# Scores of 64 features: the second of two products on 128 rows instead of 64

## The chip, the core and the metric

One core of a Trainium2 chip runs the whole program. The metric is the device time of one execution in microseconds; lower is better. The core's engines are TensorE (PE for its matmuls, PEld for its weight loads), VectorE (DVE), ScalarE (ACT), GpSimd (POOL) and SyncE (SP), which issues most transfers.

## What is computed

Two layers of a block with three token mixers side by side on 256 latent and 256 context tokens of 1024 features: a gated linear attention (GLA, 4 heads), a differential attention (8 heads) and a multi-head latent attention (MLA, 8 heads). Their gated outputs are merged and projected, and a SwiGLU feed-forward follows. The second layer produces outputs for the 256 latent tokens only. The change concerns the scores of two of the mixers:

```python
def diff_core(q, k, v, lam):
    s = jnp.einsum('bhmqd,bhmkd->bhmqk', q, k)          # m = 2 maps, d = 64
    p = jax.nn.softmax(s.astype(jnp.float32), axis=-1)
    w = p[:, :, 0] - lam * p[:, :, 1]
    return jnp.einsum('bhqk,bhkd->bhqd', w.astype(v.dtype), v)

def mla_core(q_nope, q_rope, k_nope, k_rope, v):        # d = 128 and d = 64
    s = jnp.einsum('bhqd,bhkd->bhqk', q_nope, k_nope) + jnp.einsum('bhqd,bkd->bhqk', q_rope, k_rope)
    ...
```

Latent queries see 512 keys, context queries the 256 of the context.

## The kernel before

Operands of matmuls are pairs: a float32 value is split into a high half, rounded to the matmul's type float32r, and a low half, the rest. A product of two pairs takes three matmuls into one PSUM tile, high by high, high by low and low by high (`mm3`, L234 to L236). The weights stream in by 512 KB transfers (tile `raw`); ScalarE makes their high half `wh` (L212), VectorE the low half `wl` (L213), and three tiles of each are in stock.

Scores of 64 features (both maps of a differential head; the rotary part of a latent-attention head) take two matmuls instead of three. `stack_k` lays the key's high half in one group of 64 rows and its low half in the other (tiles `ks[0]`, `ks[1]`, for the map of either group). `stack_q` lays the query's high half in both groups, twice 64 rows by ScalarE (L503, L504, tiles `qs[0]`, `qs[1]`), and its low half, by VectorE (L505), in one tile `qs[2]` in the place of its own group. `stacked` then makes the score: the first matmul (L508) contracts 128 rows and gives high by high and high by low in one; the second (L509) contracts the 64 rows of one group, the query's low half by the key's high half. In the code, q of a differential head is tag `q`, the key tag `k`; in the latent attention the query's rotary part is tag `rs` and the key's tag `qr`.

`diff_proj` and `mla_proj` project a head's operands (rotation by `rope`, L483 to L486) and call `stack_q` once for the latent tokens and, in layer 0, once more for the context; in the latent attention two heads share one call. `diff_attend` and `mla_attend` take the scores for each tile of 128 queries, then the row maximum (L721), the exponential (L723), the transposes (L732, L928) and the product with the values (L785). A differential head ends with a norm by token (L790, the power on GpSimd L178, L795) and a transpose (L798). Between the heads stand parts of the branch products (`branch_part`, eviction into U, L964), gates and the projections of the next head. The order on each engine is set by a scheduler when the program is built, from dependences, buffers and its own costs; each engine then runs its list in that order, and waits where an operand isn't there.

Of the kernel before, what the change touches and what calls it, by code (L numbers as in the profile page):

```python
# [38 lines left out]
def r32(ap):  # L39
    return ap.bitcast(F32)  # L40
# [3 lines left out]
def hybrid_block_kernel(  # L44
# [18 lines left out]
    BUFS = dict(X=3, XL=3, A=3, Y=15, U=8, M=16, acc=8, a2r=2, a2=2, early=4, xt=2, raw0=11, raw1=5, u=27, wo=33, q=6, k=6, v=16, e=6, pT=11, rt=5, mr=3, mz=8, qr=2, rs=8, gt=6, o=3)  # L63
# [26 lines left out]
    def keep(shape):  # L90
        """Columns of the store for what stays for the whole program."""
        n = math.prod(shape[1:])
        o = stored[0]
        stored[0] += n
        t = store[:, o:o + n]
        if len(shape) == 3:
            t = t.rearrange("p (a b) -> p a b", b=shape[2])
        elif len(shape) == 4:
            t = t.rearrange("p (a b c) -> p a b c", b=shape[2], c=shape[3])
        return t  # L100
# [5 lines left out]
    def small(w=1):  # L106
        """w columns for values that are needed soon and briefly."""
        o = small_n[0]
        if o + w > SMALL:
            o = 0  # L110
        small_n[0] = o + w
        return ring[:, o:o + w]
# [8 lines left out]
    # the first transfers of a queue leave in the order given here  # L121
# [35 lines left out]
    # silu(c) and silu(c_ctx) as columns, the rest of the 32 columns zero  # L157
# [17 lines left out]
    def rpow(o, v, a):  # L175
        """o = (v + a) ** -0.5 on a column."""
        ts(o, v, a, None, op0=ALU.add)  # L177
        nc.gpsimd.tensor_tensor(o, o, mhalf, op=ALU.pow)  # L178

# [1 line left out]
    def load(src, kt, n, tag=None):  # L181
        """[kt * 128, n] of a weight, at most 1024 values to a partition."""
        if tag:
            return fetch(T([P, 1024], tag), src, kt, n)
        with tc.high_priority():
            return fetch(wp.tile([P, 1024], F32, tag="raw", name=nm("raw"), bufs=4), src, kt, n)
# [11 lines left out]
    def split(v, tag=None):  # L198
        """v [128, a, b] -> hi, lo as lists of a views [128, b]: products read them by k."""
        a, b = v.shape[1], v.shape[2]  # L200
        step = a if a * b <= 512 else a // 2
        hs, ls = [], []
        with tc.high_priority():
            for o in range(0, a, step):
                n = step * b
                if tag:
                    h, lo = T([P, 512], tag, F32R), T([P, 512], tag, F32R)
                else:
                    h = wp.tile([P, 512], F32R, tag="wh", name=nm("wh"), bufs=WB)
                    lo = wp.tile([P, 512], F32R, tag="wl", name=nm("wl"), bufs=WB)  # L210
                h, lo = [t[:, 0:n].rearrange("p (k c) -> p k c", c=b) for t in (h, lo)]
                nc.scalar.copy(h, v[:, o:o + step, :])  # L212
                tt(lo, v[:, o:o + step, :], r32(h), op=ALU.subtract)  # L213
                hs += [h[:, k, :] for k in range(step)]
                ls += [lo[:, k, :] for k in range(step)]
        return hs, ls
# [4 lines left out]
    def wtiles(src, kt, cols):  # L221
        """Column ranges of a [kt * 128, .] weight side by side."""
        n = sum(b - a for a, b in cols)
        with tc.high_priority():
            raw = wp.tile([P, 1024], F32, tag="raw", name=nm("raw"), bufs=4)
            v = raw[:, 0:kt * n].rearrange("p (k c) -> p k c", c=n)
            o = 0
            for a, b in cols:
                nc.sync.dma_start(v[:, :, o:o + b - a], src[:, a:b].rearrange("(k p) c -> p k c", p=P))
                o += b - a  # L230
        return split(v)
# [6 lines left out]
    def feat_block(o, w, X, n0, n1, c0=0, m=P):  # L238
        """o[m, n] = sum_k w[k, c0:c0+m]^T X[k, n0:n1]"""
        wh, wl = w  # L240
        for k in range(KD):
            mm3(o, wh[k][:, c0:c0 + m], wl[k][:, c0:c0 + m], X[k][0][:, n0:n1], X[k][1][:, n0:n1],
                k == 0, k == KD - 1)

    def wfeat(src):
        """A [1024, 128] weight."""
        tick()
        return wtile(src, KD, P)

    def wtok(src, tag=None):  # L250
        """A [1024, 256] weight as two halves of k."""
        tick()
        tick()
        return [wtile(src[512 * j:512 * j + 512, :], 4, 256, tag) for j in range(2)]

    def tok_block(o, ws, X, t0, c0, c1):
        """o[128 tokens, c1-c0] = X[:, t0:t0+128]^T w[:, c0:c1], k in order of ws"""
# [8 lines left out]
    # chunks of w_mod: 0 sh1, 1 sc1, 2 g1, 3 sh2, 4 sc2, 5 g2  # L266
# [5 lines left out]
    def mod_load(l, ch, pc, j, tag=None):  # L272
        """512 rows of 256 columns."""
# [3 lines left out]
    def mod_first(ch, pc, raws):  # L277
        """256 columns of a chunk of layer 0, both streams, by token; eight k tiles on four column groups."""
# [10 lines left out]
    def mod_step():  # L289
        """A quarter of a piece: 512 columns of a chunk, both streams, by token; each 128 have a column group."""  # L290
# [18 lines left out]
    def mod_close():  # L309
        """Columns of mcols[l, ch], bias added (+1 for scales, /2 for gates)."""  # L310
# [43 lines left out]
    def gate_rows(l, ch, s):  # L354
        """[128 tokens, 1024] of stream s's half gate, in two tiles."""
        return bcast_row(grow[l, ch][s], "v")

# [16 lines left out]
    def modulate(src, i, l, which, X):  # L374
        """src [128, 1024] tokens of tile i -> X hi/lo columns of tile i."""
# [19 lines left out]
    class Feat:  # L395
        """Feature-major hi/lo operand of 1024 features; [k] is the pair of tile k."""
# [16 lines left out]
    def first_X():  # L413
        """The first modulated operand, feature tile by feature tile as their shifts and scales come."""
# [25 lines left out]
        # the statistics of a tile run while the power of the one before is taken  # L440
# [36 lines left out]
    def rope(pl, f=1.0):  # L477
        """pl: [128, 256] PSUM of two 64-row groups -> f times the rotated."""
# [10 lines left out]
    # scores of 64 features in two products: hi twice with hi over lo, lo with hi  # L489
    ROWS = (slice(0, 64), slice(64, 128))  # L490

    def stack_k(src, ks, c):
        """ks[m]: hi of row group m in its place, lo in the other group."""
# [5 lines left out]
    def stack_q(src, qs, c, f=1.0):  # L499
        """qs[m]: hi of row group m in both groups; qs[2]: lo in place."""  # L500
        for m in range(2):
# [3 lines left out]
            stt(qs[2][r, c], src[r, :], f, r32(qs[m][r, c]), op0=ALU.mult, op1=ALU.subtract)  # L505

    def stacked(o, m, qs, q, ks, k, start, stop):
        mm(o, qs[m][:, q], ks[m][:, k], start=start, stop=False)  # L508
        mm(o, qs[2][ROWS[m], q], ks[m][ROWS[m], k], start=False, stop=stop)  # L509
# [9 lines left out]
    def gla_gates(l, X, tag, after):  # L519
        """log-decays (x 16) of all heads: {(head, dir)}: [128, 512]."""  # L520
        # one product of 96 rows: hi and lo of the weights with hi, hi with lo
# [77 lines left out]
    def gla_attend(l, h, X, TQ, la, kqv, y):  # L599
        """TQ tokens with outputs; the context's final states serve the latent part."""  # L600
        kk, qq, vv = kqv
        # running sums: bf inclusive, cb exclusive, each stream from its own start
# [8 lines left out]
        # final states of the context  # L611
# [21 lines left out]
        # queries against those states  # L633
# [9 lines left out]
        # pair weights by halving: level g pairs the halves of blocks of 2 g tokens  # L643
# [43 lines left out]
        # outputs by token, normalised  # L687
# [15 lines left out]
        for j in range(2):  # L703
            # gate
# [32 lines left out]
    def diff_proj(l, h, X, TQ, vprev):  # L737
# [8 lines left out]
        qp = [*pair("q", TQ), T([P, 512], "q", F32R)]  # L746
# [16 lines left out]
    def diff_attend(l, h, TQ, kqv, y):  # L763
        kp, qp, vv = kqv
        j = h % 2
        if True:
            ot = T([P, 512], "o")
            on = [ot[:, P * i:P * i + P] for i in range(TQ // P)]
            for i in range(TQ // P):
# [17 lines left out]
                # o / s0, then the rms norm: the scale s0 moves into its guard  # L787
# [16 lines left out]
    def mla_front(l, X, TQ):  # L804
        """normalised q and kv latents and the rotated key part, feature-major hi/lo, by token pairs."""
# [56 lines left out]
    def mla_proj(l, h, TQ, front, prev):  # L862
# [19 lines left out]
        if j == 0:  # L882
# [3 lines left out]
            qr = [*pair("rs", TQ), T([P, 512], "rs", F32R)]  # L886
# [15 lines left out]
    def mla_attend(l, h, TQ, kr, kqv, y):  # L902
# [4 lines left out]
        for i0 in range(0, TQ // P, 2):  # L907
# [14 lines left out]
            # keys by partition, both query tiles side by side  # L922
# [24 lines left out]
    def branch_part(l, br, p, y, TQ, U):  # L947
        """U (+)= rows w p .. w p + w - 1 of a branch's product, all columns; w is 512 for the short stream."""
# [17 lines left out]
    def merge(l, br, n, X, TQ, U, acc, XM, gt):  # L966
        """acc (+)= the gated branch, both twice too large"""
# [11 lines left out]
    def residual(l, i, r, G, Bt, st):  # L979
        """r <- LN(r) * G + Bt in place; st: statistics of its four column blocks."""  # L980
# [7 lines left out]
    # what runs between the heads: branch parts, gates, the latents of the MLA branch  # L988
# [92 lines left out]
    for l in range(DEPTH):  # L1081
# [68 lines left out]
        # output projection and residual  # L1150
# [16 lines left out]
        for g in groups:  # L1167
            for cb_ in range(4) if g is groups[0] else (3, 2, 1, 0):
                # the last column blocks stay for the other tokens
# [17 lines left out]
        # feed-forward  # L1187
# [13 lines left out]
        for lo_f, hi_f in (((0, RND), (RND, 22)) if TQ == 512 else ((0, 22),)):  # L1201
# [13 lines left out]
            for part in parts:  # L1215
                for cb_ in range(4) if 0 in part else (3, 2, 1, 0):
                    tags = [t for t in ("mm", "t", "s", "o") for _ in range(PB[t])][4 * (cb_ % 2):]
                    pos = {i: ps(tags[n], [P, 256]) for n, i in enumerate(part)}
                    # the last column blocks stay for the other tokens
# [13 lines left out]
                    if last and cb_ == 3:  # L1233
                        # the first tokens end early, so that only the others' norm is left at the end
# [36 lines left out]
def _constants():  # L1271
    """Arrays that the shapes alone fix: identity, rotary tables, pair masks, row selectors."""
# [41 lines left out]
```

## Time and profile before

| | |
|---|---|
| median of 3 runs | 2157.45 us (2156.32 to 2159.31) |
| span of the profiled execution | 2154.1 us |
| TensorE matmuls busy | 2099.5 us (97%) |
| VectorE busy | 1436.7 us (67%) |
| ScalarE busy | 1076.6 us (50%) |
| differential heads, layer 0 | about 314 to 618 us |
| latent-attention heads, layer 0 | about 618 to 860 us |
| differential heads, layer 1 | about 1530 to 1760 us |
| latent-attention heads, layer 1 | about 1760 to 1860 us |

The profile is of one execution. Its span runs from the first to the last instruction; the time of a run also holds what lies around the span. Matmuls overlap, each one's end being modelled, so a busy TensorE does not say how fast it advances: that is read from the starts of successive matmuls. Idle time of an engine that others don't wait for costs nothing.

### The profile page before, as it was taken

To read this page: it belongs to the slowest core of one execution; us is meant where nothing else is said; L and a number is where in the kernel's file an instruction comes from. 1 tells how busy PE (TensorE), PEld (TensorE's weight loads), DVE (VectorE), ACT (ScalarE), POOL (GpSimd) and SP (SyncE) were. 2 spreads that over 40 slices of the span, in tenths; PEclk is the share of its full clock that TensorE was granted. 3 is DMA by queue.
4 is the path that set the end of the run, shared out by engine and by line. 5 is a ranking of instruction groups with operands and counts; after the bars stand their busy time and mean duration, and the time that the engine had idled before them with its cause. 6 is when DMAs were issued, how large, how long until landed. Compare 5 with 4: busy or idle time off the path is not lost.

```text
span 2154.1 us, 36382 instructions
## 1 busy us (share of the span) xinstructions
PE 2099.5 (97%) x14103; PEld 1812.2 (84%) x14103; DVE 1436.7 (67%) x3168; ACT 1076.6 (50%) x2495; POOL 96.0 (4%) x187
## 2 busy tenths in 40 slices
PE   7999999999999999999999999999999999998998
PEld 4888887777777778799899889988978888998998
DVE  5699657767467666685334448598566888785656
ACT  3756345666454553434231334765465676644452
POOL 0001001111000000010000000000000000000000
PEclk9999999999999999999999999999999999998999
DMA  9322343332322234627324446533434333568653
GB/s 294 102 87 69 118 99 93 86 106 60 91 81 66 78 127 137 176 84 214 104 89 127 118 127 182 159 91 118 136 88 128 106 113 85 172 191 213 172 178 116
DMA packets 349270, 268.29 MB, mean 125 GB/s; under 512 B 19932, under 2 KB 316520, under 8 KB 349096
## 3 DMA queue, kind: packets, MB, share of 16 engines
q1 hardware_dynamic: 335632, 252.22, 40.1%
q10 hardware_dynamic: 13464, 13.74, 2.1%
q8 instruction: 111, 1.82, 0.3%
q14 instruction: 63, 0.52, 0.1%
HBM read 263.79 MB, written 2.12 MB: 123 GB/s over the span
## 4 chain that ended last, share of the span: by engine, by line
PE 79%; DVE 11%; ACT 4%; issue 2%; POOL 2%; DMA 1%; ACTq 0%; DVEq 0%; POOLq 0%
PE ps_mm L234 18%; PE ps_mm L235 18%; PE ps_mm L236 18%; PE ps_s L234 3%; PE ps_s L236 3%; PE ps_s L235 3%; PE ps_s L509 3%; POOL store L178 2%; PE ps_s L508 2%; DVE wl L213 2%; PE ps_md L299 1%; PE ps_s L681 1%; DMA grow<-store 1%; ACT rt L483 1%; PE ps_t L928 1%
## 5 line engine op out<-in xcount | busy, mean ns | idle before, releaser
L213 DVE TENSOR_TENSOR wl<-raw,wh 128x512 fp32r<-128x512 f32 (+2 forms) x719 | 468.8, 674 | 139.7 <-ACT wh L212 82.4
L212 ACT CAST wh<-raw 128x512 fp32r<-128x512 f32 (+2 forms) x719 | 416.2, 611 | 254.1 <-PE ps_mm L235 135.0
L234 PE MATMUL ps_mm<-X,wh 128*128 128x512 f32 (+1 forms) x1264 | 440.8, 349 | 0.0
L235 PE MATMUL ps_mm<-XL,wh 128*128 128x512 f32 (+1 forms) x1264 | 437.4, 346 | 0.0
L236 PE MATMUL ps_mm<-X,wl 128*128 128x512 f32 (+1 forms) x1264 | 435.7, 345 | 0.0
L234 PEld LDWEIGHTS ps_mm<-X,wh 128*128 128x128 f32 x1264 | 241.2, 191 | 33.3 <-issue 7.3
L235 PEld LDWEIGHTS ps_mm<-XL,wh 128*128 128x128 f32 x1264 | 241.3, 191 | 27.3 <-issue 2.7
L236 PEld LDWEIGHTS ps_mm<-X,wl 128*128 128x128 f32 x1264 | 241.0, 191 | 26.2 <-issue 0.7
L236 PE MATMUL ps_mm<-wh,XL 128*128 128x256 f32 (+1 forms) x544 | 156.8, 292 | 0.0
L235 PE MATMUL ps_mm<-wl,X 128*128 128x256 f32 (+1 forms) x544 | 156.5, 292 | 0.1
L234 PE MATMUL ps_mm<-wh,X 128*128 128x256 f32 (+1 forms) x544 | 152.8, 294 | 0.0
L178 POOL TENSOR_TENSOR store<-store 128x1 f32<-128x1 f32 x112 | 75.6, 676 | 1657.4 <-DVE store L177 1633.9
L234 PE MATMUL ps_s<-X,wh 128*128 128x256 f32 (+1 forms) x384 | 126.2, 329 | 4.9 <-ACT wh L212 4.9
L236 PE MATMUL ps_mm<-wh,u 128*128 128x256 f32 x444 | 125.8, 283 | 0.0
L235 PE MATMUL ps_mm<-wl,u 128*128 128x256 f32 x444 | 125.6, 283 | 0.0
L234 PE MATMUL ps_mm<-wh,u 128*128 128x256 f32 x444 | 125.6, 283 | 0.0
L236 PE MATMUL ps_s<-X,wl 128*128 128x256 f32 (+1 forms) x384 | 125.1, 326 | 0.0
L235 PE MATMUL ps_s<-XL,wh 128*128 128x256 f32 (+1 forms) x384 | 125.0, 326 | 0.0
L234 PE MATMUL ps_mm<-Y,wh 128*128 128x512 f32 (+1 forms) x352 | 119.9, 341 | 0.1
L235 PE MATMUL ps_mm<-Y,wh 128*128 128x512 f32 (+1 forms) x352 | 118.6, 337 | 0.0
L236 PE MATMUL ps_mm<-Y,wl 128*128 128x512 f32 (+1 forms) x352 | 118.4, 336 | 0.0
L723 ACT ACTIVATE e<-ps_s,store 128x512 f32<-128x512 f32 (+1 forms) x144 | 88.5, 617 | 47.1 <-DVE store L721 45.4
(306 smaller groups left out, 4481.7 us busy)
## 6 DMA issues: line engine op xcount, KB each, us to landing
raw<-in_w_in_dram SPq DMA_DIRECT2D x144, 512.0 KB, 4.6
raw<-in_w_mod_dram SPq DMA_DIRECT2D x96, 512.0 KB, 3.7
raw<-in_ffn_w_in_dram SPq DMA_DIRECT2D x96, 512.0 KB, 7.1
raw<-in_w_branch_dram SPq DMA_DIRECT2D x48, 512.0 KB, 3.5
raw<-in_ffn_w_out_dram SPq DMA_DIRECT2D x46, 512.0 KB, 3.4
raw<-in_w_out_dram SPq DMA_DIRECT2D x16, 512.0 KB, 4.2
raw<-in_w_in_dram SPq DMA_DIRECT2D x16, 448.0 KB, 3.4
v<-grow ACTq DMA_DIRECT2D x12, 256.0 KB, 4.1
```

The source lines that it names most:

```text
L178: nc.gpsimd.tensor_tensor(o, o, mhalf, op=ALU.pow)
L212: nc.scalar.copy(h, v[:, o:o + step, :])
L213: tt(lo, v[:, o:o + step, :], r32(h), op=ALU.subtract)
L234: mm(o, lh, rh, start=start, stop=False)
L235: mm(o, lh, rl, start=False, stop=False)
L236: mm(o, ll, rh, start=False, stop=stop)
L299: mm(pm[32 * g:32 * g + 32, :], cst[:, 2 * j + k, :], v[:, k, P * g:P * g + P], start=(j == 0 and k == 0), stop=(j == 3 and k == 1))
L483: act(qw[a:a + 32, :], pl[b:b + 32, :], AF.Copy, scale=f)
L508: mm(o, qs[m][:, q], ks[m][:, k], start=start, stop=False)
L509: mm(o, qs[2][ROWS[m], q], ks[m][ROWS[m], k], start=False, stop=stop)
L681: mm(pa[:, i, :], kx[:, P * i:P * i + P], qx[:, P * j:P * j + P], start=True, stop=True)
L723: act(e, pscore, AF.Exp, bias=mx, accum_out=s)
```

## The change

The query's low half gets a tile for each map, `qs[2]` and `qs[3]`, and stands there in both groups of rows. The second matmul contracts all 128 rows: the query's low half by the key's high half and, new, by its low half. The tags `q` and `rs` get two buffers more each. The first matmul, the key's side and the transfers stay.

```diff
-    BUFS = dict(... q=6, ... rs=8, ...)
+    BUFS = dict(... q=8, ... rs=10, ...)
...
     def stack_q(src, qs, c, f=1.0):
         for m in range(2):
             r, o = ROWS[m], ROWS[1 - m]
             act(qs[m][r, c], src[r, :], AF.Copy, scale=f)
             act(qs[m][o, c], src[r, :], AF.Copy, scale=f)
-            stt(qs[2][r, c], src[r, :], f, r32(qs[m][r, c]), op0=ALU.mult, op1=ALU.subtract)
+            for g in (r, o):
+                stt(qs[2 + m][g, c], src[r, :], f, r32(qs[m][r, c]), op0=ALU.mult, op1=ALU.subtract)

     def stacked(o, m, qs, q, ks, k, start, stop):
         mm(o, qs[m][:, q], ks[m][:, k], start=start, stop=False)
-        mm(o, qs[2][ROWS[m], q], ks[m][ROWS[m], k], start=False, stop=stop)
+        mm(o, qs[2 + m][:, q], ks[m][:, k], start=False, stop=stop)
...
-        qp = [*pair("q", TQ), T([P, 512], "q", F32R)]
+        qp = [*pair("q", TQ), *pair("q", TQ)]
...
-            qr = [*pair("rs", TQ), T([P, 512], "rs", F32R)]
+            qr = [*pair("rs", TQ), *pair("rs", TQ)]
```

The rest of the diff takes comments out. From L506 of the changed kernel on, lines have numbers that are one higher: the subtraction is L506, the two matmuls L509 and L510.

The scheduler answers the added subtractions with another order in places. On VectorE, at the operands of the second differential head of layer 0 (`q` tiles are the query's halves, `rt` the rotated query, `ps_mm` the projection in PSUM, U the branch product, `wl` the low half of weights), before:

```order
L505 SCALAR_TENSOR_TENSOR q_3362<-ps_mm_3325,q_3360 64x256
L964 TENSOR_TENSOR U_746<-U_746,ps_mm_3411 128x512
L505 SCALAR_TENSOR_TENSOR q_3362<-rt_3363,q_3360 64x256
L964 TENSOR_TENSOR U_747<-U_747,ps_mm_3419 128x512
L505 SCALAR_TENSOR_TENSOR q_3362<-rt_3363,q_3361 64x256
L213 TENSOR_TENSOR wl_3442<-raw_3435,wh_3441 128x512
L213 TENSOR_TENSOR wl_3611<-raw_3608,wh_3610 128x512
L505 SCALAR_TENSOR_TENSOR q_3362<-ps_mm_3325,q_3361 64x256
```

and after:

```order
L506 SCALAR_TENSOR_TENSOR q_3367<-ps_mm_3330,q_3365 64x256 x2
L506 SCALAR_TENSOR_TENSOR q_3367<-rt_3369,q_3365 64x256 x2
L506 SCALAR_TENSOR_TENSOR q_3368<-rt_3369,q_3366 64x256 x2
L213 TENSOR_TENSOR wl_3452<-raw_3445,wh_3451 128x512
L506 SCALAR_TENSOR_TENSOR q_3368<-ps_mm_3330,q_3366 64x256
L213 TENSOR_TENSOR wl_3621<-raw_3618,wh_3620 128x512
L506 SCALAR_TENSOR_TENSOR q_3368<-ps_mm_3330,q_3366 64x256
L965 TENSOR_TENSOR U_746<-U_746,ps_mm_3421 128x512
L965 TENSOR_TENSOR U_747<-U_747,ps_mm_3429 128x512
```

Eight subtractions stand where four stood, and the evictions into U that stood between them now come behind.

On TensorE, at the scores of the first latent-attention head of layer 0 (three score tiles `ps_s`, the key `qr`, the query's high and low half `rs`), before:

```order
L508 MATMUL ps_s_6240<-qr_3862,rs_6187 128x512
L509 MATMUL ps_s_6240<-qr_3862,rs_6189 128x512
L508 MATMUL ps_s_6251<-qr_3862,rs_6187 128x512
L509 MATMUL ps_s_6251<-qr_3862,rs_6189 128x512
L508 MATMUL ps_s_6295<-qr_3862,rs_6187 128x256
L509 MATMUL ps_s_6295<-qr_3862,rs_6189 128x256
L234 MATMUL ps_mm_6347<-mz_3860,wh_6343 128x512
```

and after:

```order
L509 MATMUL ps_s_6285<-qr_3877,rs_6227 128x512
L509 MATMUL ps_s_6296<-qr_3877,rs_6227 128x512
L509 MATMUL ps_s_6340<-qr_3877,rs_6227 128x256
L510 MATMUL ps_s_6285<-qr_3877,rs_6229 128x512
L510 MATMUL ps_s_6296<-qr_3877,rs_6229 128x512
L510 MATMUL ps_s_6340<-qr_3877,rs_6229 128x256
L234 MATMUL ps_mm_6392<-mz_3875,wh_6388 128x512
```

The three low products, which stood each behind its high product, now stand together behind the third high product.

## Rows read from the trace of the kernel before

**Rows 1.** The page: busy time by engine, and the chain of waits by engine.

```profile
PE 2099.5 (97%) x14103; PEld 1812.2 (84%) x14103; DVE 1436.7 (67%) x3168; ACT 1076.6 (50%) x2495; POOL 96.0 (4%) x187
...
PE 79%; DVE 11%; ACT 4%; issue 2%; POOL 2%; DMA 1%; ACTq 0%; DVEq 0%; POOLq 0%
```

**Rows 2.** Busy time by stretch: window, its length, busy us (count) per engine, clock, DMA.

```profile
314.00:618.00 304.00, 298.23 (x1694) 228.16 (x1693) 208.72 (x510) 175.10 (x481) 35.75 (x72) 1.00 0.30 89
618.00:860.00 242.00, 241.49 (x1252) 190.15 (x1252) 161.69 (x326) 117.98 (x265) 0.00 (x0) 1.00 0.33 97
1530.00:1760.00 230.00, 225.84 (x1565) 192.81 (x1565) 164.31 (x378) 143.00 (x372) 18.64 (x37) 1.00 0.38 114
1760.00:1860.00 100.00, 98.60 (x663) 84.54 (x662) 83.64 (x194) 69.41 (x172) 1.47 (x3) 1.00 0.31 87
```

**Rows 3.** The chain of waits by line, in those four stretches, in their order.

```profile
by line: PE ps_mm L235 18.6%; PE ps_mm L234 18.1%; PE ps_mm L236 17.5%; PE ps_s L509 7.5%; POOL store L178 5.1%; PE ps_s L508 4.7%; PE ps_o L785 3.1%; DVE o L795 3.0%; ACT rt L483 2.2%; PE ps_md L299 1.8%; DVE pT L734 1.8%; DVE k L497 1.8%;
...
by line: PE ps_mm L234 23.5%; PE ps_mm L236 22.6%; PE ps_mm L235 22.5%; PE ps_s L509 4.9%; PE ps_t L928 4.3%; PE ps_s L234 3.2%; PE ps_s L508 2.9%; PE ps_o L234 2.8%; PE ps_o L235 2.6%; PE ps_o L236 2.3%; PE ps_s L236 2.1%; PE ps_s L235 2.0
...
by line: PE ps_mm L234 18.0%; PE ps_mm L235 17.2%; PE ps_mm L236 17.1%; PE ps_s L509 5.7%; PE ps_s L508 4.6%; ACT rt L483 3.8%; PE ps_o L785 3.2%; issue 2.2%; DVE pT L734 2.1%; DVE wl L213 2.1%; POOL store L178 2.0%; DVE k L497 1.7%; PE ps_
...
by line: PE ps_mm L234 16.3%; PE ps_mm L235 15.3%; PE ps_mm L236 15.3%; PE ps_t L928 7.0%; PE ps_s L509 6.9%; PE ps_s L508 4.9%; PE ps_o L234 4.5%; PE ps_s L236 3.9%; PE ps_o L235 3.9%; PE ps_s L235 3.6%; PE ps_s L234 3.5%; PE ps_o L236 3.3
```

**Rows 4.** Line L509, the low product: count, min/median/max ns, first and last start, forms.

```profile
L509 PE MATMUL ps_s<-k,q x96: 378/492/503, 315.3 to 1760.4; 64*128 64x512 f32 x64, 64*128 64x256 f32 x32
...
L509 PE MATMUL ps_s<-qr,rs x48: 379/492/503, 618.6 to 1852.6; 64*128 64x512 f32 x32, 64*128 64x256 f32 x16
```

**Rows 5.** Matmuls in time, 512 columns: start us, us, engine, line, tiles, rows*columns.

```profile
313.63 0.39 PE L234 MATMUL ps_mm<-Y,wh 128*128 128x512 f32 x1
...
314.99 0.39 PE L508 MATMUL ps_s<-k,q 128*128 128x512 f32 x1
315.31 0.50 PE L509 MATMUL ps_s<-k,q 64*128 64x512 f32 x1
315.74 0.49 PE L508 MATMUL ps_s<-k,q 128*128 128x512 f32 x1
...
317.45 0.50 PE L234 MATMUL ps_mm<-X,wh 128*128 128x512 f32 x1
317.79 0.40 PE L235 MATMUL ps_mm<-XL,wh 128*128 128x512 f32 x1
```

**Rows 6.** The same view, where score pairs have 256 columns.

```profile
320.25 0.28 PE L508 MATMUL ps_s<-k,q 128*128 128x256 f32 x1
...
320.77 0.50 PE L236 MATMUL ps_mm<-X,wl 128*128 128x512 f32 x1
321.10 0.39 PE L234 MATMUL ps_mm<-X,wh 128*128 128x512 f32 x1
```

**Rows 7.** All engines in time, before the first latent-attention scores.

```profile
617.64 0.40 DVE L505 SCALAR_TENSOR_TENSOR rs<-ps_mm,rs 64x256 fp32r<-64x256 f32 x1
...
618.07 0.28 PE L235 MATMUL ps_s<-k,q 128*128 128x256 f32 x1
...
618.18 0.28 PE L236 MATMUL ps_s<-k,q 128*128 128x256 f32 x1
...
618.30 0.40 PE L508 MATMUL ps_s<-qr,rs 128*128 128x512 f32 x1
```

**Rows 8.** Line L553, a product of 96 rows and 512 columns.

```profile
L553 PE MATMUL ps_s<-e,a x16: 392/395/446, 66.9 to 1384.5; 96*128 96x512 f32 x16
```

**Rows 9.** Matmuls in time, two low products side by side.

```profile
427.25 0.50 PE L509 MATMUL ps_s<-k,q 64*128 64x512 f32 x2
```

**Rows 10.** VectorE by line and form: busy us, mean ns, idle before.

```profile
L497 DVE TENSOR_TENSOR k<-rt,k 64x256 fp32r<-64x256 f32 x32 | 13.4, 419 | 0.8
L505 DVE SCALAR_TENSOR_TENSOR q<-rt,q 64x256 fp32r<-64x256 f32 x32 | 13.3, 417 | 6.2 <-ACT q L503 5.9
```

**Rows 11.** Who TensorE waited for, 314 to 618 us: total us, times, longest.

```profile
PE ps_t L798 <- DVE o L795: 3.3, 11, 0.7
```

More of the change, by code (lines that the diff above doesn't have):

```diff
@@ L61, in nm @@
         return f"{s}_{uid[0]}"
-    BUFS = dict(X=3, XL=3, A=3, Y=15, U=8, M=16, acc=8, a2r=2, a2=2, early=4, xt=2, raw0=11, raw1=5, u=27, wo=33, q=6, k=6, v=16, e=6, pT=11, rt=5, mr=3, mz=8, qr=2, rs=8, gt=6, o=3)
+    BUFS = dict(X=3, XL=3, A=3, Y=15, U=8, M=16, acc=8, a2r=2, a2=2, early=4, xt=2, raw0=11, raw1=5, u=27, wo=33, q=8, k=6, v=16, e=6, pT=11, rt=5, mr=3, mz=8, qr=2, rs=10, gt=6, o=3)
     def T(shape, tag, dtype=F32):
```

## The prediction, on record before the changed kernel ran

> **What bounds the kernel now.** I read the busy table first, then the stretches in which the changed products run, then the chain of waits, and last the matmuls one by one. TensorE is busy for 97% of the span, VectorE for 67% [rows 1]. The changed products lie in four stretches: the differential heads of layer 0 (314 to 618 us), its latent-attention heads (618 to 860), and the same two of layer 1 (1530 to 1760, 1760 to 1860). In each, TensorE is idle for 5.8, 0.5, 4.2 and 1.4 us, some 12 us in all, and VectorE is busy for 208.7 of 304, 161.7 of 242, 164.3 of 230 and 83.6 of 100 us [rows 2]. So TensorE sets the pace there, and the only stretch in which VectorE comes near it is the last (84%). The chain of waits agrees: the low product of the scores (L509) alone holds 7.5%, 4.9%, 5.7% and 6.9% of these stretches [rows 3], that is 22.8 + 11.9 + 13.1 + 6.9 = 54.7 us.
>
> **What the low product costs now.** There are 96 + 48 = 144 of them, all of 64 rows; 96 have 512 columns, 48 have 256 [rows 4]. A busy TensorE hides their price, since matmuls overlap; it is seen from start to start. Six 128-row products of 512 columns in a row start 1.36 us apart in all, 0.227 each (313.63 to 314.99). Then three score pairs (high product L508, low product L509) follow: 314.99, 315.31, 315.74, and so on to 317.45, and the matmul behind them starts its successor at 317.79 [rows 5]. These seven intervals take 2.80 us where seven at 0.227 would take 1.59. So 1.21 us are lost over three pairs, 0.40 a pair. With 256 columns: the intervals from 320.25 to 321.10 take 0.85 us [rows 6]; two products of 256 columns start 0.23 us apart in all (618.07 to 618.30, [rows 7]), so these two and one of 512 would take 0.46, and 0.39 us is lost. The loss lies on both sides of the 64-row product: it starts 0.1 us late, the product behind it 0.2 us late, the next 0.1.
>
> Is it the short contraction? A product of 96 rows and 512 columns lasts 395 ns [rows 8], like the 128-row ones in [rows 5], while a 64-row one lasts 492 [rows 4]. So it isn't; what costs is going from products on the whole array to one on a half and back. The new low product has 128 rows, reads the same key tile as the high product before it and writes the same bank; I take 0.227 and 0.115 us for it, as for every 128-row product.
>
> **The sum on TensorE.** In layer 0 each differential head scores two latent query tiles against 512 keys and two context tiles against 256, twice (64 products, half and half); the latent-attention heads do it once (32, half and half); layer 1 has 32 + 16, all against 512. So 96 x 0.403 + 48 x 0.39 = 57.4 us. By stretch that is 25.4, 12.7, 12.9 and 6.4 us. At three places two low products stand next to each other and share the way there and back; one is shown in [rows 9]. They lose some 1.2 us less, so 56 us.
>
> One more row bears on this. At 427.25 us two low products, of the two row groups, take 0.50 us together [rows 9]. The Trainium skill, TensorEngine Tiling (Array Packing), Key Properties, says that tiles of the array work independently and that different tiles can run matmuls in parallel; by it the way to use 64-row products is to set two of different groups side by side, and the change, against that rule, gives it up. The trace agrees at that place, but two 128-row products take 2 x 0.227 = 0.45 us, which is no more; and the order of the kernel before sets them so at one place of 144, so the sum stays at 56 us.
>
> **What it adds on VectorE.** The query's low half is written to both row groups: four subtractions (L505, now L506) instead of two for each call of stack_q. There are 72 now, of 0.417 us [rows 10], and 72 more come, 30.2 us; the order of the changed kernel shows the doubled rows. The new ones read one row group and write the other. The row nearest to that is L497 of the key, which does just this in 0.419 us [rows 10], so they are no dearer. By stretch: 32 x 0.42 = 13.4, 6.7, 6.7 and 3.4 us. With TensorE's saving taken off the stretch, VectorE would be busy for 222 of 279 us (80%), 168 of 229 (73%), 171 of 217 (79%) and 87 of 93.5 us (93%). So the added work lies beside TensorE's, except where VectorE is itself on the chain: it holds 11% of the whole chain [rows 1], so 30.2 x 0.11 = 3 us, with 0 and 30 us as the ends. What is queued behind the new rows is the splitting of the next weights (L213) and the evictions into U, as the order shows in the second head; TensorE waits for those when VectorE falls behind by more than the three split tiles that are in stock. ScalarE gets no work, and no transfer moves; the added buffers (two of tag q, two of tag rs) cost no time.
>
> At the first latent-attention head all four of the first subtractions come before the low products. In the trace the first of them starts at 617.64; two more behind it end by 617.64 + 3 x 0.42 = 618.9, and the three high products from 618.30 on end their starts at 618.30 + 0.57 = 618.87 [rows 7]. So hardly a wait there.
>
> **What is late next.** With the scores done earlier, TensorE comes to the steps that hang on the softmax sooner. The longest of its waits now is for the normalised outputs of the differential heads (L798 for L795): 3.3 us over 11 in the first stretch [rows 11]. All its waits in the four stretches come to 12 us. Lower end: none grow, since VectorE and ScalarE start the softmax sooner too. Upper end: in the differential heads half the saving is waited away, (25.4 + 12.9) / 2 = 19 us. I take 8 us, nearer to the waits that are there than to the upper end, because both sides of that chain move forward.
>
> **The forecast.** -56 + 3 + 8 = -45 us. The profiled execution has a span of 2154.1 us; the median of the runs is 2157.45, so 3.4 us lie outside the span, and they stay. 2154.1 - 45 + 3.4 = **2112.5 us**, 2.1% faster.
>
> **Rivals.**
> (a) The softmax chain takes over in the differential heads: 19 us of waits instead of 8, and 10 us of VectorE's rows on the chain. -56 + 19 + 10 = -27, **2130 us**. For it: in these heads the chain also runs through L795, L734 and the one-column powers of GpSimd (POOL store L178, 5.1%, [rows 3]). Against it: TensorE waits only 5.8 of 304 us there [rows 2].
> (b) VectorE becomes the bound: all 30.2 us exposed, -56 + 30 = -26, **2131 us**. For it: 93% in the last stretch. Against it: that stretch holds only 3.4 us of the added work; elsewhere a fifth of VectorE's time is left.
> (c) The new order also removes some of the 12 us of waits: all 57 us and a few more, **2095 us**.
> (d) Slower: the price isn't the half array but the second product itself, that is reading the same keys again into the same bank. Then the second product still costs 0.40 us with 128 rows, TensorE saves nothing, and VectorE adds its 30.2 us, a third of which would be exposed next to a TensorE that is as slow as now: **2167 us**. It decides if the matmul behind the new low product still starts 0.43 us after it. Against it: the three products of mm3 also fill one bank, the third (L236 at 618.18) reads the key tile of the first again, and they keep 0.115 us [rows 7].
> (e) Next to no change: a small saving and small waits cancel, **2157 us**; nothing in the profile calls for it.
>
> **Chances.** The forecast, from 36 to 57 us saved: 0.68. (a) 0.13, (b) 0.07, (c) 0.05, (d) 0.04, (e) 0.03. A measurement of this kernel tells changes of about 0.2% (4 us) from none. Faster by more: 0.68 + 0.13 + 0.07 + 0.05 = 0.93; within: 0.03; slower: 0.04. The range takes in the full saving with nothing lost and a little luck (2157.45 - 59 = 2098) and (a) and (b) at its upper end, 2131.
>
> **What would show it.** Right: the low product on 128 rows, starting 0.227 us after the high one, and the matmul behind it 0.227 later; the four stretches shorter by about 23, 12, 10 and 5 us, nothing changed elsewhere; 144 subtractions of 0.42 us; VectorE near 80% in the differential heads, near 93% in the last stretch; TensorE's waits in the four stretches at about 20 us instead of 12. Wrong: starts still 0.3 to 0.43 us apart around the low product (d); waits of 30 us or more at L798, L785 and L732, now one line further down (a); waits of TensorE for the splits of L213 (b).

## The result, and the profile after

| | before | after |
|---|---|---|
| median | 2157.07 us | 2119.92 us (4 runs, 2118.81 to 2120.92) |
| span of the profiled execution | 2154.1 us | 2117.7 us |
| ratio of the times | | 0.9828 (95% interval 0.9817 to 0.984) |

The kernel became 1.7% faster: 37 us were gained, 45 had been forecast. The time is inside the range and 7.4 us above the forecast.

The first view is the page: busy time by engine, and the chain of waits by engine.

```profile
PE 2052.3 (97%) x14103; PEld 1808.8 (85%) x14103; DVE 1461.3 (69%) x3240; ACT 1073.1 (51%) x2495; POOL 98.2 (5%) x187
...
PE 77%; DVE 12%; ACT 5%; issue 2%; POOL 2%; DMA 1%; ACTq 0%; DVEq 0%; POOLq 0%; SPq 0%
```

Against [rows 1] TensorE's matmuls lost 47 us of busy time, VectorE gained 25 us and 72 instructions, and VectorE's share of the chain of waits rose by a point. The next view is the matmuls in time (start us, us, engine, line, tiles, rows*columns), at the scores that [rows 5] and [rows 6] show of before; L509 is now the high product, L510 the low one.

```profile
315.92 0.39 PE L509 MATMUL ps_s<-k,q 128*128 128x512 f32 x1
316.14 0.39 PE L510 MATMUL ps_s<-k,q 128*128 128x512 f32 x1
316.37 0.39 PE L509 MATMUL ps_s<-k,q 128*128 128x512 f32 x1
316.60 0.39 PE L510 MATMUL ps_s<-k,q 128*128 128x512 f32 x1
...
317.27 0.39 PE L234 MATMUL ps_mm<-X,wh 128*128 128x512 f32 x1
...
319.54 0.28 PE L509 MATMUL ps_s<-k,q 128*128 128x256 f32 x1
319.65 0.28 PE L510 MATMUL ps_s<-k,q 128*128 128x256 f32 x1
319.77 0.40 PE L236 MATMUL ps_mm<-X,wl 128*128 128x512 f32 x1
```

High and low products start 0.227 us apart, and the matmul behind a pair 0.227 us after it. With 256 columns it is 0.11 to 0.12 us. At these places no trace is left of the 0.40 us that a pair lost.

The rows of the weight loads (PEld) show what the loss went with. In the kernel before, at the first pair of [rows 5]:

```profile
314.77 0.19 PEld L508 LDWEIGHTS ps_s<-k,q 128*128 128x128 f32 x1
315.31 0.18 PEld L509 LDWEIGHTS ps_s<-k,q 64*128 64x128 f32 x1 [0.35 <-issue]
315.74 0.19 PEld L508 LDWEIGHTS ps_s<-k,q 128*128 128x128 f32 x1 [0.25 <-issue]
```

The load for the 128-row product at 314.99 starts 0.22 us ahead of it; the load for the 64-row product at 315.31 starts with it, and so does the next one, for the 128-row product at 315.74. Over all 144 low products the median lead of the load is 0.002 us before the change and 0.223 us after it.

In the chain of waits of the first stretch the change reads so (line by line, shares of the stretch):

```profile
by line: PE ps_mm L234 17.8%; PE ps_mm L235 17.6%; PE ps_mm L236 17.3%; POOL store L178 5.3%; PE ps_o L786 4.3%; PE ps_s L509 3.6%; PE ps_s L510 3.5%; DVE o L796 3.0%; ACT rt L483 2.8%; issue 2.4%; PE ps_md L299 2.4%; DVE k L497 2.1%; ACT e
```

L509 and L510 now hold about the same there, where the low product held 7.5% against 4.7% of the high one [rows 3].

For a comparison by stage I cut each trace at the same matmuls: the first score product of the differential heads of a layer, the first of its latent-attention heads, and the first eviction of the output projection behind these (L1158 of before), so that the latent-attention stages also hold what stands between the heads and that projection. Busy time in these four stages, in the columns of [rows 2] (length, then busy us of PE, PEld, DVE, ACT, POOL), before:

```profile
314.99:618.30 303.31, 297.54 (x1691) 227.66 (x1690) 208.03 (x509) 174.67 (x481) 35.75 (x72) 1.00 0.31 89
618.30:908.29 289.99, 284.22 (x1487) 225.27 (x1486) 190.09 (x371) 138.74 (x302) 0.00 (x0) 0.99 0.37 108
1565.91:1770.49 204.58, 199.38 (x1349) 167.24 (x1348) 152.47 (x353) 131.53 (x345) 18.04 (x37) 1.00 0.34 103
1770.49:1918.56 148.07, 147.94 (x1087) 135.45 (x1088) 118.41 (x259) 95.95 (x224) 0.55 (x1) 1.00 0.52 154
```

and after:

```profile
315.92:600.53 284.61, 276.13 (x1691) 226.17 (x1690) 217.22 (x537) 173.73 (x481) 36.09 (x72) 1.00 0.34 96
600.53:882.51 281.98, 272.93 (x1485) 223.03 (x1484) 195.00 (x388) 137.50 (x302) 0.00 (x0) 0.99 0.38 111
1541.08:1735.50 194.42, 187.66 (x1349) 167.75 (x1347) 156.96 (x367) 131.16 (x345) 19.84 (x37) 1.00 0.37 110
1735.50:1882.85 147.35, 144.84 (x1087) 135.53 (x1088) 122.06 (x267) 95.16 (x224) 0.55 (x1) 1.00 0.54 156
```

The stages became 18.7, 8.0, 10.2 and 0.7 us shorter, 37.6 us in all; the rest of the program is 1.3 us longer. TensorE's idle time in them (length less PE busy) rose from 5.8 + 5.8 + 5.2 + 0.1 = 16.9 us to 8.5 + 9.0 + 6.8 + 2.5 = 26.8. So the score products became as cheap as forecast, and part of the gain came back as waiting.

### The profile page after: what moved, and what is told of

Same layout as the page of the kernel before. It is cut to its first block, busy times and chain, and to the rows that moved or that the text cites. A ratio compares the mean times of both kernels' runs of the same rounds, so it can differ in the third digit from the quotient of the medians.

```text
span 2117.7 us, 36478 instructions
## 1 busy us (share of the span) xinstructions
PE 2052.3 (97%) x14103; PEld 1808.8 (85%) x14103; DVE 1461.3 (69%) x3240; ACT 1073.1 (51%) x2495; POOL 98.2 (5%) x187
## 4 chain that ended last, share of the span: by engine, by line
PE 77%; DVE 12%; ACT 5%; issue 2%; POOL 2%; DMA 1%; ACTq 0%; DVEq 0%; POOLq 0%; SPq 0%
PE ps_mm L234 18%; PE ps_mm L235 18%; PE ps_mm L236 18%; PE ps_s L234 3%; PE ps_s L236 3%; PE ps_s L235 3%; POOL store L178 2%; DVE wl L213 2%; PE ps_md L299 2%; PE ps_s L682 1%; ACT rt L483 1%; PE ps_s L509 1%; PE ps_s L510 1%; PE ps_o L786 1%; ACT wh L212 1%
## 5 line engine op out<-in xcount | busy, mean ns | idle before, releaser
L213 DVE TENSOR_TENSOR wl<-raw,wh 128x512 fp32r<-128x512 f32 (+2 forms) x719 | 468.4, 674 | 143.1 <-ACT wh L212 70.7
```

## Experiments

**Theories.** T1, that of the forecast: the gain is the end of the 64-row products (56 us), the waits take back some 8 us, and the added work of VectorE is nearly free (3 us). T2: the added subtractions cost far more than 3 us, because TensorE waits for VectorE. T3, the rival (d): it isn't the rows of the second product that cost. Eight kernels tell them apart. Some compute what the kernel before computes, some also low by low, like the changed one. The kernel before ran beside them, with 2156.84 us (e1, e2, e3, e6) and 2156.01 us (e5, e7, e8, e9).

The scheduler orders each kernel anew, so a run differs from its neighbour in the order of some instructions too; no run holds the order fixed. All results in one table: the change of each stage against before, in us, read from the same landmarks in each trace. Differential heads are D0 and D1, latent-attention heads M0 and M1, for the two layers.

| kernel | median us | ratio (95%) | D0 | M0 | D1 | M1 | elsewhere |
|---|---|---|---|---|---|---|---|
| after | 2119.92 | 0.9828 (0.9817 to 0.984) | -18.7 | -8.0 | -10.2 | -0.7 | +1.3 |
| e1_zero | 2111.12 | 0.9792 (0.9777 to 0.9806) | -20.4 | -11.0 | -11.2 | -2.7 | +0.4 |
| e2_dve_only | 2167.39 | 1.0051 (1.0034 to 1.0068) | +2.2 | +3.6 | +1.1 | +2.4 | +1.6 |
| e3_side_by_side | 2138.23 | 0.9918 (0.9903 to 0.9932) | -14.8 | +2.6 | -7.6 | +1.0 | +1.6 |
| e5_pool_copy | 2111.60 | 0.9793 (0.9778 to 0.9807) | -20.5 | -10.6 | -10.7 | -2.9 | -0.2 |
| e6_ring1 | 2131.41 | 0.9891 (0.9876 to 0.9905) | -17.4 | -7.2 | -11.4 | -2.8 | +14.0 |
| e7_diff_only | 2129.03 | 0.9876 (0.986 to 0.9893) | -18.9 | +0.4 | -10.2 | 0.0 | +0.7 |
| e8_mla_zero | 2114.39 | 0.9807 (0.9792 to 0.9821) | -18.8 | -12.1 | -10.2 | -2.6 | +0.8 |
| e9_zero_early | 2114.25 | 0.9804 (0.9789 to 0.9818) | -20.1 | -10.8 | -10.8 | -2.4 | 0.0 |

**e2: the subtractions alone.** The added subtractions of VectorE stay, the 64-row product comes back.

```diff
-        mm(o, qs[2 + m][:, q], ks[m][:, k], start=False, stop=stop)
+        mm(o, qs[2 + m][ROWS[m], q], ks[m][ROWS[m], k], start=False, stop=stop)
```

> VectorE's part of the change alone: the low half is written to both row groups, but the second product reads the 64 rows of one group as before. Theory A: TensorE is slower here than in the changed kernel and hides more of the added 30 us, so 2158 to 2165 us. Theory B: 2156 to 2159 us, as before. If the second product, and not its 64 rows, were what costs, the changed kernel's gain would have another cause and show here: 2120 us.

It took 10.5 us more than the kernel before, more than any of the expectations allowed; 9.3 of them lie in the four stages, 6.0 in the two of the latent attention, which hold 24 of the 72 added instructions. So VectorE's work costs 10 us, not 3, on a TensorE that is as slow as before. The forecast had this price, a third of the added work, in its rival (d), and this run came at that rival's time. And what the changed kernel gains over this one, 47.5 us, is the 128-row product alone: T3 falls, since by it the two would be equal.

**e1: zeros instead.** The low half stands only in its own group, the other group is set to zero by GpSimd, and the product still runs over 128 rows. VectorE has the work of before.

```diff
-            for g in (r, o):
-                stt(qs[2 + m][g, c], src[r, :], f, r32(qs[m][r, c]), op0=ALU.mult, op1=ALU.subtract)
+            nc.gpsimd.memset(r32(qs[2 + m][o, c]), 0.0)
+            stt(qs[2 + m][r, c], src[r, :], f, r32(qs[m][r, c]), op0=ALU.mult, op1=ALU.subtract)
```

> The changed kernel with the low half subtracted into its own row group only, as before the change, and zeros set by GpSimd in the other group; the second product keeps 128 rows. It computes what the kernel before computes. VectorE's 72 added subtractions are gone, TensorE's side of the change stays. Theory A (TensorE gains about 48 us from the 128 rows, and some 10 us of that are lost to VectorE's added work): faster than the changed kernel, 2107 to 2113 us. Theory B (the lost part is the wait on the softmax chain alone, VectorE's added work costs nothing): as the changed kernel, 2118 to 2122 us.

This kernel is 8.8 us faster than the changed one, and 45.7 us faster than the kernel before. It is, with e5, the fastest of the study and computes what the kernel before computes. The work that VectorE gave up stands on GpSimd, as the groups of its page show (engine, operation, tile, shape, count, then busy us and mean ns of one; what comes behind is idle time before them):

```profile
L505 POOL MEMSET q<- 64x256 f32 x48 | 13.8, 305 | 1.7
L505 POOL MEMSET rs<- 64x256 f32 x24 | 7.1, 312 | 179.4 <-PE ps_o L236 94.6 <-DVE k L515 42.2 <-PE ps_mm L235 40.7
```

These are 20.9 us on an engine that is busy for 5% of the span. Its four stages, in the columns of before:

```profile
314.83:597.73 282.90, 275.62 (x1691) 226.15 (x1690) 206.20 (x509) 173.97 (x481) 44.62 (x104) 1.00 0.35 97
597.73:876.73 279.00, 272.47 (x1483) 223.45 (x1482) 188.48 (x372) 137.50 (x302) 3.77 (x14) 0.99 0.40 113
1536.03:1729.37 193.34, 187.62 (x1349) 167.80 (x1347) 151.12 (x353) 130.58 (x345) 22.20 (x53) 1.00 0.37 109
1729.37:1874.75 145.38, 144.28 (x1087) 136.05 (x1088) 118.13 (x259) 95.49 (x224) 2.38 (x7) 1.00 0.54 158
```

In them e1 against after gives the price of VectorE's work once more: 1.7, 3.0, 1.1 and 2.0 us, 7.7 in all (by the unrounded lengths), and again most of it, 4.9, in the latent attention.

**e5: a copy by GpSimd.** Does it matter that the second place is filled later, or that VectorE fills it? Here it is filled with the low half, as in the changed kernel, but by a copy of GpSimd behind VectorE's subtraction.

```diff
-            for g in (r, o):
-                stt(qs[2 + m][g, c], src[r, :], f, r32(qs[m][r, c]), op0=ALU.mult, op1=ALU.subtract)
+            stt(qs[2 + m][r, c], src[r, :], f, r32(qs[m][r, c]), op0=ALU.mult, op1=ALU.subtract)
+            nc.gpsimd.tensor_copy(qs[2 + m][o, c], r32(qs[2 + m][r, c]))
```

> The changed kernel, with the second place of the low half copied by GpSimd from the first instead of subtracted again by VectorE; it computes what the changed kernel computes. If it is VectorE's time that the added subtractions cost: as the run with zeros, 2109 to 2114 us. If it is their lateness, that is the longer way from the projection to the second product, the copy lengthens that way further: 2118 to 2124 us.

```profile
L506 POOL CAST q<-q 64x256 fp32r<-64x256 f32 x48 | 25.9, 545 | 120.6 <-DVE q L505 106.3 <-issue 13.1 <-POOL store L178 0.8
...
L506 POOL CAST rs<-rs 64x256 fp32r<-64x256 f32 x24 | 9.9, 415 | 202.6 <-DVE rs L505 189.2 <-PE ps_t L929 12.5 <-PE ps_t L799 0.9
```

Its copies start behind the subtractions and take 0.42 to 0.55 us, and the kernel is as fast as with zeros (2111.60 and 2111.12). The expectation took the second place to be later than in the changed kernel. It isn't: it is ready 0.64 us behind the first subtraction on average, against 0.74 there, since there the second subtraction often waits for its turn on VectorE (for the context's queries of the latent attention the medians are 0.50 and 1.14). What the run shows is that a second place that comes 0.64 us behind the first costs no more than zeros, which don't wait for the subtraction. So most of the 8 to 9 us goes with the work on VectorE; that none of it is lateness isn't shown for the latent attention's context.

**e7 and e8: where VectorE's time counts.** e7 changes the differential heads only; the latent attention keeps three tiles and its 64-row product.

```diff
...
-            qr = [*pair("rs", TQ), *pair("rs", TQ)]
+            qr = [*pair("rs", TQ), T([P, 512], "rs", F32R)]
```

`stack_q` and `stacked` do as before where they are given three tiles.

> The change in the differential heads alone; the latent-attention heads keep their 64-row product and one low half. From the stretches of the changed kernel (differential heads 18.7 and 10.2 us shorter, latent-attention heads 8.0 and 0.8): 2126 to 2131 us. If the latent-attention heads' share were not worth its subtractions at all: 2118 to 2121 us.

Its differential heads are those of the changed kernel (-18.9 and -10.2), its latent attention that of before (+0.4 and 0.0). So the stages don't act upon each other here, and the latent attention's part of the change is worth 9.1 us against 18.7 (12.6 + 6.1) that its low products cost. e8 puts zeros there alone, and leaves the doubled subtraction to the differential heads.

```diff
...
-            stack_q(rope(pq[:, 0:256]), qr, slice(0, 256))
+            stack_q(rope(pq[:, 0:256]), qr, slice(0, 256), zeros=True)
...
-                stack_q(pq[:, 256:512], qr, slice(256, 512))
+                stack_q(pq[:, 256:512], qr, slice(256, 512), zeros=True)
```

> The changed kernel with zeros by GpSimd instead of the second subtraction in the latent-attention heads alone (24 of the 72 added subtractions gone; there it computes what the kernel before computes). If the added work costs most where VectorE is on the path to a short projection, as the stretches of the runs with and without it say (3.0 + 1.9 us of 7.7 there): 2114 to 2116 us. If each subtraction costs the same: 24 of 72 of 9 us, 2117 us.

It gains 5.5 us on the changed kernel with a third of the subtractions taken away (four runs, 2112.84 to 2116.17, all below the 2117 of an equal price for each). A wait that the forecast missed can be read in the trace. In the latent attention the context's half of the query is subtracted straight from the projection in PSUM (`rs<-ps_mm`). All engines in time after the first latent-attention scores of layer 0, in the changed kernel (in brackets the idle time before an instruction, and what ended it):

```profile
603.09 0.43 DVE L506 SCALAR_TENSOR_TENSOR rs<-ps_mm,rs 64x256 fp32r<-64x256 f32 x1
...
603.54 0.69 DVE L213 TENSOR_TENSOR wl<-raw,wh 128x512 fp32r<-128x512 f32 x1
...
604.27 0.43 DVE L506 SCALAR_TENSOR_TENSOR rs<-ps_mm,rs 64x256 fp32r<-64x256 f32 x1
...
604.73 0.42 DVE L515 TENSOR_TENSOR v<-ps_mm,v 128x256 fp32r<-128x256 f32 x1
...
604.75 0.50 PE L234 MATMUL ps_mm<-mz,wh 128*128 128x512 f32 x1 [1.57 <-DVE rs L506]
```

The second subtraction that reads the projection's tile stands behind the splitting of a weight (L213, 0.69 us), and the tile comes free at 604.70. TensorE, which needs it for the next projection, had been idle for 1.57 us. Among TensorE's waits of this stage (us in total, times, longest) it is the largest new one:

```profile
PE ps_mm L234 <- ACT M L514: 5.3, 2, 2.8
PE ps_mm L234 <- DVE rs L506: 1.6, 1, 1.6
PE ps_s L510 <- DVE rs L506: 0.8, 1, 0.8
PE ps_mm L234 <- DVE v L515: 0.4, 1, 0.4
```

With the wait at the scores (0.8) and the one for the values (0.4) that makes 2.8 us, about the 3.0 us by which e1 is shorter there; e1 has none of the three, and the kernel before, like all of them, has the wait for M. In e2, with the slower TensorE, the first and the third are there too:

```profile
PE ps_mm L234 <- DVE rs L506: 1.2, 1, 1.2
PE ps_mm L234 <- DVE v L515: 1.1, 2, 0.8
```

**e9: zeros once a tile.** One memset where the tile is made (64 x 512 in layer 0), instead of two of 64 x 256 in `stack_q`: are the zeros on a path?

```diff
...
-        qp = [*pair("q", TQ), *pair("q", TQ)]
+        qp = cleared([*pair("q", TQ), *pair("q", TQ)])
...
```

> As the run with zeros, but one GpSimd instruction a tile, written ahead of the subtractions and of the projection's rotation, so that the zeros wait for nothing but the tile: half as many GpSimd instructions in layer 0. If the zeros were late anywhere there: 2105 to 2109 us; if they were hidden: as that run, 2109 to 2113 us.

2114.25 us; no faster than e1, and above both ranges. Each of its four stages is within 0.5 us of e1's, so the zeros of e1 cost nothing that this could take away; the 3 us between the medians are not explained.

**e6: zeros once for all.** Two fixed tiles hold the low halves of all heads, and their zeros are set once at the start. The tags `q` and `rs` have six and eight buffers again.

```diff
...
-        qp = [*pair("q", TQ), *pair("q", TQ)]
+        qp = [*pair("q", TQ), *lows(TQ)]
...
```

> As the run with zeros, but the low halves live in two fixed tiles whose zeros are set once at the start, so neither VectorE nor GpSimd gets work for them; the price is that a head's low halves can't be written before the last head's products have read them. Theory A: 2105 to 2113 us if that wait is hidden, up to 2125 if it isn't. Theory B: 2118 to 2125 us.

It took 2131.41 us, above every range that was expected. It was meant to show what it costs when a head must wait for the tile of the last one. It doesn't: 13 us are lost before the first differential head, where none of these tiles is in use. TensorE's longest wait there, up to 330 us, is:

```profile
PE ps_s L690 <- DVE gt L718: 8.5, 1, 8.5
```

No row of the kernel before has this wait. Behind it TensorE's granted clock is 0.56 from 115.3 to 125.0 us, so for most of that stretch it is at the lower of its two levels, 1.2 GHz; the kernel before has 1.00 from 100 to 150 us. By an estimate from these numbers, 9.7 us at 0.56 lose 4.3 us, which with the wait comes to 12.8 of the 13. The fixed tiles changed the order of TensorE's products in the GLA stage, where e1 has that of the kernel before. In the four stages e6 is 6.5 us behind e1, and how much of that is the fixed tiles' wait is left open by this run.

**e3: 64 rows, side by side.** The kernel before, with one thing changed: in the differential heads both maps' high products come first, then both low products, of the two row groups, next to each other.

```diff
...
-                for m in range(2):
-                    sc = ps("s", [P, 512])[:, 0:n]
-                    stacked(sc, m, qp, slice(P * i, P * i + P), kp, slice(P * a, P * b), True, True)
-                    es.append(softmax_e(sc, n))
+                qc, kc = slice(P * i, P * i + P), slice(P * a, P * b)
+                if True:
+                    scs = [ps("s", [P, 512])[:, 0:n] for m in range(2)]
+                    tail.pop("s", None)
+                    for m in range(2):
+                        chain("s", mm(scs[m], qp[m][:, qc], kp[m][:, kc], start=True, stop=False))
+                    for m in range(2):
+                        chain("s", mm(scs[m], qp[2][ROWS[m], qc], kp[m][ROWS[m], kc], start=False, stop=True))
+                    for m in range(2):
+                        es.append(softmax_e(scs[m], n))
...
```

> The kernel before with another order only: in the differential heads the two maps' high products stand first, then their two 64-row low products next to each other (in all 48 cases), which use different row groups. If the price is the way to the half array and back, and two row groups run at the same time, a pair of pairs loses 0.40 us instead of 0.80 and gives back 0.23 (0.12 with 256 columns) by the overlap: 32 x 0.63 + 16 x 0.50 = 28 us on TensorE, of which some is lost since the second score tile must be free earlier: 2130 to 2145 us. If the 64 rows cost by themselves: 2155 to 2160 us.

```profile
316.89 0.61 PE L778 MATMUL ps_s<-k,q 128*128 128x512 f32 x2
317.44 0.50 PE L780 MATMUL ps_s<-k,q 64*128 64x512 f32 x2
317.87 0.50 PE L778 MATMUL ps_s<-k,q 128*128 128x512 f32 x1
318.20 0.39 PE L234 MATMUL ps_mm<-X,wh 128*128 128x512 f32 x1
```

Two low products take 0.50 us together (317.44), and the next matmul starts 0.43 us after the first of them. The way to the half array and back is paid once for two products and not for each. That gives 18.6 us without any work on VectorE, half of what the change gains, in 96 of the 144 products. The Trainium skill, TensorEngine Tiling (Array Packing), Key Properties, says that different tiles can run matmuls in parallel; the trace agrees, in all 48 pairs the two start within 0.01 us. But each pair still pays the way there and back, and two 128-row products, 2 x 0.227 us, are no longer than two 64-row ones side by side; with 256 columns they are shorter (0.23 us against 0.31 to 0.34). By stage the differential heads gain 22.4 us here; the rest of the program, which wasn't changed, gets 5.2 us longer, and this run doesn't show why.

## Why the prediction was right, and where its size was off

**The loss at the low product: right.** The price of 56 us was read at two places and multiplied. Summed over all 144 low products of the trace of before (from the matmul ahead of each to the second one behind it, from start to start, less 0.227 us for 512 columns, 0.120 for 256 and 0.111 for 128) it is 25.1, 12.6, 13.1 and 6.1 us in the four stages, 56.9 us. Reckoned in the same way, the changed kernel has 6.8 us at its low products, 2.3 of them waits for other engines, so some 50 us of the loss are gone; e2 against after confirms that it is the rows.

**Given back behind the saving: 8 forecast as waits, 11.6 measured.** e1 has the whole saving and no work added to VectorE. Its stages are 45.3 us shorter, so 56.9 - 45.3 = 11.6 us were given back. It isn't the differential heads' chain alone, as the forecast had it: by stage it is 4.7, 1.6, 1.9 and 3.4 us. The wait that it named did grow, but little, from 3.3 us [rows 11] to 4.0 (L799 for L796):

```profile
PE ps_t L799 <- DVE o L796: 4.0, 13, 0.8
PE ps_o L786 <- DVE pT L735: 2.4, 4, 0.9
```

Of the 11.6 us, 3.8 are idle time of TensorE in the stages of e1 (7.3 + 6.5 + 5.7 + 1.1 = 20.6 us against 16.9). The rest lies in intervals in which the modelled end of one matmul covers the start of the next, 4.0 us of it at e1's low products; which engine held them the views don't say, and that stays open. So as idle time the term was 3.8 us, below the 8 of the forecast, and what lifts it to 11.6 isn't shown to be waiting. The forecast's sign of it, about 20 us of idle time in its four stretches instead of 12, came true in the changed kernel (21.2 from 316 to 842 and 1541 to 1825), but in part by luck: 6.2 of the 9.9 us of new idle time go with VectorE's added work (26.8 us against 20.6 in e1).

**VectorE's added work: 3 forecast, 8 to 10.** This is the step that failed most. The price of one was right, with 0.42 us:

```profile
L506 DVE SCALAR_TENSOR_TENSOR q<-rt,q x64: 406/420/425, 295.6 to 1718.5; 64x256 fp32r<-64x256 f32 x64
L506 DVE SCALAR_TENSOR_TENSOR q<-ps_mm,q x32: 409/423/428, 295.1 to 544.7; 64x256 fp32r<-64x256 f32 x32
L506 DVE SCALAR_TENSOR_TENSOR rs<-rt,rs x32: 406/420/425, 600.2 to 1808.7; 64x256 fp32r<-64x256 f32 x32
L506 DVE SCALAR_TENSOR_TENSOR rs<-ps_mm,rs x16: 406/422/428, 599.9 to 744.3; 64x256 fp32r<-64x256 f32 x16
```

What was wrong is the 11%, VectorE's share of the whole chain, taken for every place. e1 against after gives 8.8 us, e2 against before 10.5. In the differential heads the 48 added instructions, 20.1 us of work, cost 2.8 to 3.3 us by stage, 14 to 16%: there the share was nearly right. In the latent attention 24 of them, 10.1 us of work, cost 4.9 to 6.0 us, half or more. The forecast looked for the readers of the new tiles. There it was right: at 600.53 the three high products of the first head start, and the low ones follow at 601.12 without a wait; only one low product of that stage waited, for 0.8 us. It didn't look at what the added instructions read, a PSUM tile that is held until the last of them, nor at what they push back on VectorE. The waits of that one stage show both; how much of the price is the other order of the instructions isn't separated.

**The stages.** Forecast 23, 12, 10 and 5 us, measured 18.7, 8.0, 10.2 and 0.7. The four forecasts add up to 50, 5 us more than the forecast's own sum of 45. The last is furthest off in proportion. VectorE at 93% had been named as its danger; from 1725 to 1825 us, the stretch that matches the forecast's, it is busy for 88.1 of 100 us, over the whole stage for 122.1 of 147.4 (83%), and TensorE, which waits for nothing there before, now waits for VectorE and ScalarE:

```profile
PE ps_o L234 <- ACT pT L514: 0.9, 2, 0.5
PE ps_s L234 <- DVE Y L515: 0.7, 1, 0.7
PE ps_s L234 <- ACT e L724: 0.5, 1, 0.5
```

e1 keeps only the first of the three, and is 2.0 us shorter in this stage. That even e1 gets only 2.7 of the 6.1 us there is 1.0 us of idle time; the rest isn't explained.

**The rivals.** (a), waits of 30 us at the softmax chain, and (b), all of VectorE's 30 us exposed, are not seen: the waits for L796 and L735 in the first stage come to 6.4 us, those for the splits of L213 to 0.9 in the whole span. (c), no waits at all, falls with the 10 us of new idle time. (d) falls with the starts 0.227 us apart.

**The sum.** Forecast -56 + 8 + 3 = -45. Measured in the stages -56.9 + 11.6 + 7.7 = -37.6, and +1.3 elsewhere: -36.3 us of span. Both sizes that were too small, by 3.6 and 4.7 us, point the same way. The medians give -37.15: the profile of before is of an execution about 1 us faster than the median, since only 1.7 to 1.9 us lie outside the span wherever both times of one execution are on record (2119.53 and 2117.7), and not 3.4 as the forecast had it. That changes nothing in its sum, where the 3.4 only leads back to the median.

## What to carry to other kernels

Where a matmul on half of the array stands between matmuls on the whole, measure from start to start what the way there and back costs; filling the idle half, even with zeros, can be cheaper than leaving it out, and setting two halves side by side gets part of it. Give the filling to an engine that nobody waits for: here GpSimd's zeros got 46 us where VectorE's second copy got 37. And price added work at the place where it stands, by what it reads and holds as well as by what waits for its output, not by its engine's share of the whole chain.

## What the runs showed of the hardware that was not expected

A zero operand is enough. The 128-row product with 64 rows of zeros takes 0.227 us from start to start, like any other, where the 64-row product between 128-row ones takes 0.40 us more in all (0.1 ahead of it, 0.2 behind it, 0.1 behind the next matmul). Two 64-row products of different row groups next to each other run together, 0.50 us for both. And on VectorE writing into the other row group costs next to nothing: the rows of `q<-rt`, half of which do so, have a mean of 0.419 us, against 0.417 before [rows 10]. GpSimd set 64 x 256 values to zero in 0.305 us and copied them in 0.415 to 0.545 us (rough, as all spans on GpSimd are in these profiles), at no cost to the engines beside it that these runs could show.
